# Taking the adding transfers out of the first MLP: every low half of its weights made by VectorE

## The chip, the core and the metric

One core of a Trainium2 chip runs the whole program. The metric is the device time of one execution, in microseconds (us), as the median over several executions. The engines are named as in the profile: PE (TensorE matmuls), PEld (TensorE weight loads), DVE (VectorE), ACT (ScalarE), POOL (GpSimd), SP (SyncE, which here only issues transfers).

## What is computed

The reference runs two two-layer transformer-like blocks one after the other on a sequence of 256 tokens of width 1024, all in float32. The part that matters here is the MLP of the first layer of the first block:

```python
h = rms_norm(x, norm_mlp[layer]) * (1.0 + scale2) + shift2
x = x + gate2 * (jnp.square(jax.nn.relu(h @ mlp_w1[layer])) @ mlp_w2[layer])
```

`mlp_w1` is 1024 x 4096 and `mlp_w2` is 4096 x 1024. The shifts, scales and gates of later layers come from `mod = c_act @ ada_w[layer] + ada_b[layer]`, whose dot products the kernel computes in between.

## The kernel before, in words

**Two halves of every number.** A matmul operand is held as a high half (float32 rounded to the type `fp32r`) and a low half (what the rounding lost). A product is the sum of three matmuls: high weight by high input, high weight by low input, low weight by high input. The low half of a weight is the loaded weight minus its high half.

**Weights.** They arrive in units of 128 x 2048 floats (1 MB), in one fixed order (`weight_plan`), through six buffers `raw0` to `raw5`. SP issues the loads in program order (`pump`, L369, L378), each into a buffer that was released (`release`, L392). `unit_ahead` (L397) splits a unit into a ring of three pairs of tiles: ACT writes the high half (`wh0` to `wh2`), DVE subtracts and writes the low half (`wl0` to `wl2`, L422, through the helper at L314), and then the raw buffer is released. So the ring lets a unit be split while PE still works on the two units ahead of it.

**Adding transfers.** For seven units of the first MLP (`DMALO`, L43: the units 0, 2, ... 12 of the second weight) the low half is made in another way (L407 to L413): ACT writes the high half, releases the raw buffer, writes minus the high half into the `wl` tile, and POOL issues a transfer that reads the weights from device memory a second time and adds them into that tile (L411).

**The first MLP** (`mlp`, L951, tag `m1`). `A(u)` multiplies the input by 256 columns of the first weight (48 matmuls) into PSUM. DVE then reduces two columns (`wb`, L334) and scales and shifts the result into `ht` (L327), ACT takes relu, square and the high half `hh`, DVE the low half `hl`. `B(u)` multiplies `hh` and `hl` by 256 rows of the second weight (48 matmuls, `rows_mm`, L506), summing over all u. PE's order is A0, A1, B0, A2, B1, A3, ..., A15, B13, and then B14 with B15 and the final evacuation. A unit that is split by an adding transfer is multiplied with `late=True`: all 32 matmuls with the high weights first, and then the 16 with the low weights.

**Side work.** While the MLP runs, DVE also computes 24 dot products of the modulation (`ada_next`, L687; two for each 1 MB unit, which are read from the same six raw buffers) and tables for a later state-space layer (`s5_tables`, `s5_turns`). They have a lower priority than the MLP's work. The order of the instructions on PE, DVE and ACT in this stage is set by a scheduler when the program is built; SP and POOL keep the program's order. Each engine runs its instructions in that order, and one that waits holds up all behind it.

Of the kernel before, what the change touches and what calls it, by code (L numbers as in the profile page):

```python
# [10 lines left out]
F32 = mybir.dt.float32  # L11
F32R = mybir.dt.float32r
U8 = mybir.dt.uint8
AF = mybir.ActivationFunctionType
# [6 lines left out]
ADD, SUB, MUL, MAX, MIN = ALU.add, ALU.subtract, ALU.mult, ALU.max, ALU.min  # L21

T = 256
D = 1024
NK = D // 128
# [13 lines left out]

DMALO = {("m1b", u) for u in range(0, 14, 2)}  # L43
S5SEQ = "g P0 P1 g T0 T1 TB0 M0 P2 P3 TB1 Q0 Q1 T2 T3 g Q2 Q3"


# [227 lines left out]
class Prog:  # L274
# [122 lines left out]
    def unit_ahead(self, ahead, between=None):  # L397

        last = min(self.used_n + ahead, len(self.wseq) - 1)
        while self.split_n <= last:  # L400
            j = self.wseq[self.split_n]
            if j not in self.slot:
                assert self.split_n > self.used_n, ("not loaded", self.plan[j][1])
                break
            b = self.split_n % len(self.hb)
            raw = self.raw_of(j)
            if self.plan[j][1] in DMALO:  # L407
                self.act(self.hb[b], raw, AF.Copy)
                self.release(j)
                self.act(self.lb[b], self.hb[b].bitcast(F32), AF.Copy, scale=-1.0)  # L410
                self.nc.gpsimd.dma_start(out=self.lb[b], in_=self.a["wst"][self.wpos[j]], accum_op=ADD)  # L411
                self.split_n += 1
                continue  # L413
            n = 1 + (self.plan[j][1][0] in HALVES)
            parts = [slice(i * 2048 // n, (i + 1) * 2048 // n) for i in range(n)]
            for c in parts:
                self.act(self.hb[b][:, c], raw[:, c], AF.Copy)
            if between is not None:
                between()
                between = None  # L420
            for c in parts:
                self.tt(self.lb[b][:, c], raw[:, c], self.hb[b][:, c].bitcast(F32), SUB)  # L422
            self.release(j)
            self.split_n += 1
        if between is not None:
            between()
# [76 lines left out]
                wh, wl = (t[:, k, m * 128:(m + 1) * 128] for t in (hv, lv))  # L503
                self.pair(outs[m], wh, wl, self.X2[S][:, k], k == 0, k == NK - 1)

    def rows_mm(self, units, xs, banks, start, stop, evac=None, late=False):  # L506

        kt = [(h, l, j) for h, l in units for j in range(2)]
        out = lambda m: self.pb[banks[m // 2]][:, (m % 2) * T:(m % 2 + 1) * T]
        if evac is not None:  # L510
            fin, a, b = evac
        if late:
            for q, m in [(q, m) for q in range(2) for m in range(NK)]:
                h, l, j = kt[q]
                w = h[:, j * D + m * 128:j * D + (m + 1) * 128]
                self.mm(out(m), w, xs[q][0], q == 0 and start and m % 2 == 0, False)
                self.mm(out(m), w, xs[q][1], False, False)
            for q, m in [(q, m) for q in range(2) for m in range(NK)]:
                h, l, j = kt[q]
                self.mm(out(m), l[:, j * D + m * 128:j * D + (m + 1) * 128], xs[q][0], False, q == 1 and stop and m % 2 == 1)  # L520
            return
        for m in range(NK):
            o = out(m)
            for q, (h, l, j) in enumerate(kt):
                c = j * D + m * 128
                xh, xl = xs[q]
                wh, wl = h[:, c:c + 128], l[:, c:c + 128]
                self.mm(o, wh, xh, q == 0 and start and m % 2 == 0, False)
                self.mm(o, wh, xl, False, False)
                self.mm(o, wl, xh, False, q == len(kt) - 1 and stop and m % 2 == 1)  # L530
            if evac is not None and m % 2 == 1:
                for i in (m - 1, m):
                    fin(i, out(i))
                    a(i)
                    if i:
                        b(i - 1)
        if evac is not None:
            b(NK - 1)
# [412 lines left out]
    def mlp(self, tag, S, finish, side=(), after=None, before=None):  # L951
        n = DFF // 256
        with self.tc.tile_pool(name="pm" + tag, bufs=1) as p:
            hh = [p.tile([128, 2, T], F32R, name=f"hh{i}") for i in range(3)]
            hl = [p.tile([128, 2, T], F32R, name=f"hl{i}") for i in range(3)]
            tt_ = [p.tile([128, 2, T], F32, name=f"ht{i}") for i in range(2)]
            wb = [p.tile([128, 2], F32, name=f"wb{i}") for i in range(2)]
            yb = (0, 1, 2, 3)

            def A(u):  # L960
                b = 4 + 2 * (u % 2)
                t = s = tt_[u % 2]
                ps = [self.pb[b], self.pb[b + 1]]
                self.proj_T((tag + "a", u), S, ps, n=258, parts=1 + (u == 0))
                if u == 0:
                    self.stats(6, std=True, r2=True)
                w = wb[u % 2]
                self.red(w, self.pball[:, b:b + 2, 256:258], ADD)
                for m in range(2):
                    self.stt(t[:, m, :], self.stdb, w[:, m:m + 1], ps[m][:, :T], MUL, ADD)  # L970
                self.act(t, t, AF.Relu)
                self.act(s, t, AF.Square)
                self.act(hh[u % 3], s, AF.Copy)
                self.tt(hl[u % 3], s, hh[u % 3].bitcast(F32), SUB)

            def B(us, fin=None):
                ws = [self.unit((tag + "b", u), ahead=2 - i) for i, u in enumerate(us)]
                xs = [(hh[u % 3][:, j, :], hl[u % 3][:, j, :]) for u in us for j in range(2)]
                self.rows_mm(ws, xs, yb, us[0] == 0, us[-1] == n - 1, fin, (tag + "b", us[0]) in DMALO)

            def sides(b):
                self.side_banks = (b, b + 1)
                for one in side:

                    while one:
                        g, budget = one[0]
                        start, said = self.vcost, "more"
                        while said == "more" and self.vcost - start <= budget:
                            said = next(g, "end")
                        if said != "end":  # L990
                            break
                        one.pop(0)

            A(0)
            for u in range(1, n - 1):
                A(u)
                sides(6 - 2 * (u % 2))
                if u == n - 2:
                    A(n - 1)
                B([u - 1])  # L1000
                sides(4 + 2 * (u % 2))
            for one in side:
                for g, _ in one:
                    for _ in g:
                        pass
            if after is not None:
                after()
            if before is not None:
                before()
            B([n - 2, n - 1], finish)  # L1010

    def mlp_finish(self, gate, nxt):
# [826 lines left out]
```

## Time and profile before

| | |
|---|---|
| median of 3 runs | 1299.5 us (1299.23 to 1301.8) |
| profiled execution, its own time | 1300.48 us |
| its span, first to last instruction | 1298.7 us |
| DVE, ACT busy over the span | 1006.0 us (77%), 693.4 us (53%) |
| first MLP, from PE's first matmul of its statistics to the first evacuation | 171.4 to 363.4 us |
| bytes of the adding transfers | 7.34 MB of 291.18 MB |

The profile is one execution on the chip. Its page gives the busy time of each engine and the costliest groups of instructions; the waits name who waited for whom; the timeline gives single instructions with the idle time before them; the windows give busy time and the granted TensorE clock (1.00 is 2.4 GHz, 0.50 is 1.2 GHz) in chosen stretches. Instructions overlap slightly at their ends, so what one takes from its engine is read from the start of one to the start of the next.

### The profile page before, as it was taken

How to read it: one execution, taken by the hardware profiler on the slowest of the kernel's cores; microseconds unless marked ns; L12 is line 12 of the kernel's file. 1: busy time of each engine (PE TensorE's matmuls, PEld its weight loads, DVE VectorE, ACT ScalarE, POOL GpSimd, SP SyncE). 2: the span in 40 equal slices, each digit the busy share in tenths (PEclk: the TensorE clock that was granted, in tenths of full speed). 3: DMA queues.
4: the chain of work that ended last, by engine and by line, in shares of the span. 5: the costliest groups of instructions: out<-in, count | busy, mean ns of one | idle time of the engine just before them, and what ended most of it. 6: DMA issues, size and time to landing. Idle time of an engine off the chain costs nothing.

```text
span 1298.7 us, 22539 instructions
## 1 busy us (share of the span) xinstructions
PE 1223.4 (94%) x9412; PEld 1136.2 (87%) x9412; DVE 1006.0 (77%) x1391; ACT 693.4 (53%) x891; POOL 91.5 (7%) x80
## 2 busy tenths in 40 slices
PE   2999989989998999999999799999999999999997
PEld 1999889989998889999999589887889999888886
DVE  7899989867799997899966756667656886877553
ACT  4545466655755885545554345455445554655442
POOL 0012120000020002000001204000000000100000
PEclk7999999999999999999999899999999999999999
DMA  9877579887875564888879795354545533455510
GB/s 383 330 269 282 212 260 310 269 291 248 278 277 227 200 248 170 314 280 284 257 268 223 150 378 186 138 185 163 212 179 211 193 114 131 161 181 183 219 68 33
DMA packets 64662, 291.18 MB, mean 224 GB/s; under 512 B 8112, under 2 KB 26032, under 8 KB 32048
## 3 DMA queue, kind: packets, MB, share of 16 engines
q1 hardware_dynamic: 63552, 282.40, 60.8%
q0 software_dynamic: 1008, 7.34, 2.8%
q8 instruction: 74, 1.21, 0.4%
q14 instruction: 28, 0.23, 0.1%
HBM read 275.04 MB, written 14.68 MB: 223 GB/s over the span
## 4 chain that ended last, share of the span: by engine, by line
PE 62%; DVE 18%; ACT 8%; DMA 7%; issue 4%; POOL 1%; DVEq 0%; ACTq 0%; POOLq 0%; SPq 0%
PE psall L337 61%; DMA wl<-in_wst_dram 7%; DVE wl L314 6%; ACT wh L294 4%; DVE raw L687 3%; PE psall L340 1%; DVE tmpn L327 1%; ACT wl L294 1%; DVE sqt L327 1%; DVE X L327 1%; DVE adaacc L314 1%; ACT X L294 1%; DVE td L314 1%; POOL sqat L565 1%; DVE tmpn L314 0%
## 5 line engine op out<-in xcount | busy, mean ns | idle before, releaser
L337 PE MATMUL psall<-X,wh 128*128 128x256 f32 (+2 forms) x3360 | 727.2, 308 | 28.7 <-ACT wh L294 21.4
L337 PEld LDWEIGHTS psall<-X,wh 128*128 128x128 f32 x3360 | 542.7, 191 | 68.0 <-ACT wh L294 21.8
L337 PE MATMUL psall<-X,wl 128*128 128x256 f32 (+1 forms) x1992 | 557.3, 283 | 5.6 <-DVE wl L314 5.6
L314 DVE TENSOR_TENSOR wl<-raw,wh 128x2048 fp32r<-128x2048 f32 (+1 forms) x225 | 410.4, 1841 | 104.7 <-ACT wh L294 99.6
L294 ACT ACTIVATE wh<-raw 128x2048 fp32r<-128x2048 f32 (+1 forms) x232 | 354.4, 1546 | 205.7 <-PE psall L337 183.4
L337 PEld LDWEIGHTS psall<-X,wl 128*128 128x128 f32 x1992 | 376.2, 190 | 12.0 <-DVE wl L314 11.2
L337 PE MATMUL psall<-hh,wl 128*128 128x256 f32 x512 | 130.9, 291 | 11.5 <-DMA wl<-in_wst_dram 11.5
L337 PE MATMUL psall<-hh,wh 128*128 128x256 f32 x512 | 140.5, 285 | 0.0
L337 PE MATMUL psall<-hl,wh 128*128 128x256 f32 x512 | 140.0, 283 | 0.4 <-DVE hl L314 0.4
L337 PE MATMUL psall<-hid,wh 128*128 128x512 f32 (+1 forms) x432 | 136.3, 372 | 0.0
L565 POOL TENSOR_TENSOR sqat<-sqat,sqt 128x256 f32<-128x256 f32 x52 | 56.5, 1087 | 886.3 <-ACT sqt L294 885.1
L337 PE MATMUL psall<-hid,wl 128*128 128x256 f32 x384 | 108.0, 281 | 0.3 <-DVE wl L314 0.3
L337 PEld LDWEIGHTS psall<-hh,wl 128*128 128x128 f32 x512 | 92.2, 196 | 14.1 <-DMA wl<-in_wst_dram 12.9
L337 PEld LDWEIGHTS psall<-hl,wh 128*128 128x128 f32 x512 | 97.9, 192 | 0.6 <-DVE hl L314 0.6
L337 PEld LDWEIGHTS psall<-hh,wh 128*128 128x128 f32 x512 | 97.6, 191 | 0.5 <-issue 0.4
L337 PEld LDWEIGHTS psall<-hid,wh 128*128 128x128 f32 x432 | 78.1, 189 | 15.4
L687 DVE CUSTOM_DVE_ANT_0 raw<-raw,adaacc,prmt 128x1024 f32<-128x1024 f32 x64 | 81.2, 1292 | 4.3 <-DMA raw<-in_wst_dram 4.3
L337 PEld LDWEIGHTS psall<-hid,wl 128*128 128x128 f32 x384 | 72.6, 189 | 0.6 <-DVE wl L314 0.6
L294 ACT ACTIVATE tmpn<-psall 128x256 f32<-128x256 f32 (+1 forms) x38 | 17.7, 465 | 62.1 <-PE psall L337 62.1
L314 DVE TENSOR_TENSOR tmpn<-tmpn,psall 128x256 f32<-128x256 f32 (+1 forms) x32 | 17.6, 552 | 38.0 <-ACT tmpn L294 38.0
L294 ACT ACTIVATE ht<-ht 128x512 f32<-128x512 f32 x64 | 39.9, 625 | 12.4 <-DVE ht L327 11.9
L687 DVE CUSTOM_DVE_ANT_0 raw<-raw,adaacc,adn 128x1024 f32<-128x1024 f32 x32 | 42.1, 1338 | 4.2 <-ACT td L294 4.2
(346 smaller groups left out, 1256.8 us busy)
## 6 DMA issues: line engine op xcount, KB each, us to landing
raw<-in_wst_dram SPq DMA_DIRECT2D x231, 1024.0 KB, 5.8
wl<-in_wst_dram POOLq DMA_DIRECT2D x7, 1024.0 KB, 12.6
dQ<-s5X SPq DMA_DIRECT2D x8, 512.0 KB, 4.8
dP<-s5X SPq DMA_DIRECT2D x16, 256.0 KB, 5.6
s5X<-in_wst_dram SPq DMA_DIRECT2D x4, 1024.0 KB, 14.3
raw<-dK SPq DMA_DIRECT2D x32, 128.0 KB, 9.5
s5X<-in_s5blk_dram SPq DMA_DIRECT2D x8, 256.0 KB, 3.8
s5X<-dP SPq DMA_DIRECT2D x2, 1024.0 KB, 8.0
```

What stands on the lines that cost most here:

```text
L294: i = self.nc.scalar.activation(out=out, in_=in_, func=func, **kw)
L314: return self.nc.vector.tensor_tensor(out=out, in0=a, in1=b, op=op)
L327: return self.nc.vector.scalar_tensor_tensor(out=out, in0=a, scalar=s, in1=b, op0=op0, op1=op1)
L337: return self.in_bank(out, self.nc.tensor.matmul(out, lhsT=l, rhs=r, start=start, stop=stop))
L340: return self.in_bank(out, self.nc.tensor.transpose(out, in_, self.ident))
L565: self.nc.gpsimd.tensor_tensor(out=self.sqa, in0=self.sqa, in1=s, op=ADD)
L687: self.nc.vector.tensor_tensor_reduce(out=w, in0=w, in1=self.crow, scale=1.0 if sc is None else sc, scalar=b, op0=MUL, op1=ADD, accum_out= ...
```

## The change

The set `DMALO` and the branch that serves it are removed, so the seven units take the ordinary way: ACT writes the high half, DVE subtracts, and the raw buffer is released after DVE's subtraction. With it go the argument `late` and its order of matmuls.

```diff
-DMALO = {("m1b", u) for u in range(0, 14, 2)}
...
-            if self.plan[j][1] in DMALO:
-                self.act(self.hb[b], raw, AF.Copy)
-                self.release(j)
-                self.act(self.lb[b], self.hb[b].bitcast(F32), AF.Copy, scale=-1.0)
-                self.nc.gpsimd.dma_start(out=self.lb[b], in_=self.a["wst"][self.wpos[j]], accum_op=ADD)
-                self.split_n += 1
-                continue
...
-    def rows_mm(self, units, xs, banks, start, stop, evac=None, late=False):
+    def rows_mm(self, units, xs, banks, start, stop, evac=None):
...
-        if late:
-            for q, m in [(q, m) for q in range(2) for m in range(NK)]:
-                h, l, j = kt[q]
-                w = h[:, j * D + m * 128:j * D + (m + 1) * 128]
-                self.mm(out(m), w, xs[q][0], q == 0 and start and m % 2 == 0, False)
-                self.mm(out(m), w, xs[q][1], False, False)
-            for q, m in [(q, m) for q in range(2) for m in range(NK)]:
-                h, l, j = kt[q]
-                self.mm(out(m), l[:, j * D + m * 128:j * D + (m + 1) * 128], xs[q][0], False, q == 1 and stop and m % 2 == 1)
-            return
...
-                self.rows_mm(ws, xs, yb, us[0] == 0, us[-1] == n - 1, fin, (tag + "b", us[0]) in DMALO)
+                self.rows_mm(ws, xs, yb, us[0] == 0, us[-1] == n - 1, fin)
```

The scheduler then orders this stage anew on PE, DVE and ACT; before and after the stage the orders are the same, and SP's is the same throughout. POOL loses its seven transfers in the stage. Line numbers in the changed kernel are smaller, by 2 (L312 for L314) up to 19.

PE at one of the seven units (B2, split into `wh0` and `wl0`; `hh2` and `hl2` are its inputs), before, at its end and the start of the next unit:

```order
L337 MATMUL psall_61<-hh2_1486,wh0_73 128x256
L337 MATMUL psall_61<-hl2_1489,wh0_73 128x256
L337 MATMUL psall_61<-hh2_1486,wl0_76 128x256 x16
L337 MATMUL psall_61<-X00_171,wh1_74 128x258
L337 MATMUL psall_61<-X00_171,wh1_74 128x256
L337 MATMUL psall_61<-X00_171,wl1_77 128x258
```

and now, at its start:

```order
L335 MATMUL psall_61<-X00_171,wl2_78 128x258
L335 MATMUL psall_61<-X00_171,wh2_75 128x258
L335 MATMUL psall_61<-X00_171,wh2_75 128x256
L335 MATMUL psall_61<-X00_171,wl2_78 128x258
L335 MATMUL psall_61<-hh2_1486,wh0_73 128x256
L335 MATMUL psall_61<-hl2_1489,wh0_73 128x256
L335 MATMUL psall_61<-hh2_1486,wl0_76 128x256
```

The low half was needed after 32 matmuls of its unit, and is now needed by the third.

ACT around the same kind of unit (B4, in `wh1`), before, with the relu and the square of the unit before it in `ht0`:

```order
L294 ACTIVATE wh1_74<-raw1_68 128x2048
L294 ACTIVATE ht0_1490<-ht0_1490 128x512
L294 ACTIVATE wl1_77<-wh1_74 128x2048
L294 ACTIVATE ht0_1490<-ht0_1490 128x512
L294 ACTIVATE hh1_1485<-ht0_1490 128x512
L294 ACTIVATE wh2_75<-raw0_67 128x2048
```

and now:

```order
L292 ACTIVATE wh1_74<-raw1_68 128x2048
L292 ACTIVATE ht0_1490<-ht0_1490 128x512 x2
L292 ACTIVATE hh1_1485<-ht0_1490 128x512
L292 ACTIVATE wh2_75<-raw0_67 128x2048
L292 ACTIVATE wh0_73<-raw4_71 128x2048
```

The copy with the sign changed is gone from between the two steps on `ht0`.

DVE from the reduction after A8 on (`wb0`), before; `ISA raw` is a dot product of the modulation, `ISA mod` its short second part, `wl1_77<-raw2_69` the low half for A10:

```order
L334 TENSOR_REDUCE wb0_1492<-psall_61 128x2
L687 ISA raw1_68,mod1_1_123<-raw1_68,adaacc1_136,adn1_1_130,prmt_88 128x1024
L687 ISA mod1_1_123 128x1
L327 SCALAR_TENSOR_TENSOR ht0_1490<-stdbt_106,wb0_1492,psall_61 128x256 x2
L687 ISA raw4_71,mod1_0_122<-raw4_71,adaacc1_136,prmt_88 128x1024
L687 ISA mod1_0_122 128x1
L687 ISA raw4_71,mod1_0_122<-raw4_71,adaacc1_136,prmt_88 128x1024
L687 ISA mod1_0_122 128x1
L314 TENSOR_TENSOR hl2_1489<-ht0_1490,hh2_1486 128x512
L314 TENSOR_TENSOR wl1_77<-raw2_69,wh1_74 128x2048
```

and now:

```order
L332 TENSOR_REDUCE wb0_1492<-psall_61 128x2
L325 SCALAR_TENSOR_TENSOR sqt_102<-adaacc0_135,sqt_102 128x512
L325 SCALAR_TENSOR_TENSOR ht0_1490<-stdbt_106,wb0_1492,psall_61 128x256 x2
L312 TENSOR_TENSOR wl0_76<-raw5_72,wh0_73 128x2048
L312 TENSOR_TENSOR hl2_1489<-ht0_1490,hh2_1486 128x512
L325 SCALAR_TENSOR_TENSOR tmpn_103<-adaacc0_135,tmpn_103 128x512
L668 ISA raw0_67,mod1_1_123<-raw0_67,adaacc1_136,adn1_1_130,prmt_88 128x1024
L668 ISA mod1_1_123 128x1
L312 TENSOR_TENSOR sqt_102<-sqt_102,tmpn_103 128x512
L668 ISA raw1_68,mod1_1_123<-raw1_68,adaacc1_136,adn1_1_130,prmt_88 128x1024
L668 ISA mod1_1_123 128x1
L312 TENSOR_TENSOR wl1_77<-raw2_69,wh1_74 128x2048
```

The added low half of B8 (`wl0_76<-raw5_72`) stands here, and side work that stood ahead of this reduction (the second dot product of `raw0`, the table steps on `sqt` and `tmpn`) now stands behind it.

## Rows read from the trace of the kernel before

**Rows 1.** The page, first part: busy us (share of the span) x instructions.

```profile
PE 1223.4 (94%) x9412; PEld 1136.2 (87%) x9412; DVE 1006.0 (77%) x1391; ACT 693.4 (53%) x891; POOL 91.5 (7%) x80
```

**Rows 2.** Windows: first MLP, its first part, then the second MLP (two stretches).

```profile
core 0: us, PE busy (x) PEld busy (x) DVE busy (x) ACT busy (x) POOL busy (x), PEclk, DMA share, GB/s
171.40:363.40 192.00, 179.87 (x1440) 177.99 (x1441) 151.92 (x276) 117.57 (x114) 6.33 (x8) 0.97 0.86 285
171.40:271.10 99.70, 92.79 (x733) 91.51 (x734) 85.12 (x179) 58.07 (x58) 3.76 (x5) 0.97 0.85 278
...
540.00:640.00 100.00, 100.00 (x879) 96.06 (x878) 97.84 (x95) 52.57 (x61) 0.00 (x0) 1.00 0.84 285
523.90:695.00 171.10, 171.10 (x1491) 165.32 (x1490) 146.64 (x148) 88.81 (x104) 0.00 (x0) 1.00 0.86 274
```

**Rows 3.** PE's waits, 165 to 372 us: us in total, times, longest.

```profile
PE psall L337 <- DMA wl<-in_wst_dram: 11.5, 7, 2.7
...
PE psall L337 <- DVE hl L314: 0.4, 1, 0.4
PE psall L337 <- DVE wl L314: 0.3, 1, 0.3
```

**Rows 4.** Chain of waits that ended last, 230 to 272 us: start, us, what.

```profile
222.25 12.86 DMA wl<-in_wst_dram
...
235.16 9.33 PE psall L337 x63
...
246.94 1.82 ACT wl L294
```

**Rows 5.** PE's timeline at two of the seven waits: start, us, group [idle before].

```profile
235.16 3.19 PE L337 MATMUL psall<-hh,wl 128*128 128x256 f32 x16 [2.01 <-DMA wl<-in_wst_dram]
...
339.82 2.17 PE L337 MATMUL psall<-hh,wl 128*128 128x256 f32 x16 [2.02 <-DMA wl<-in_wst_dram]
```

**Rows 6.** Windows at three stretches of low clock (columns as in rows 2).

```profile
235.96:239.36 3.40, 3.40 (x18) 3.40 (x17) 1.77 (x4) 3.32 (x4) 0.00 (x0) 0.50 0.87 349
263.60:266.70 3.10, 3.10 (x17) 3.10 (x17) 2.28 (x2) 0.00 (x0) 0.00 (x0) 0.51 0.44 172
290.20:293.90 3.70, 3.70 (x21) 3.70 (x21) 1.77 (x2) 1.92 (x3) 0.00 (x0) 0.54 1.01 423
```

**Rows 7.** DVE's timeline around A7's reduction: start, us, instruction.

```profile
255.03 1.34 DVE L687 CUSTOM_DVE_ANT_0 raw<-raw,adaacc,adn 128x1024 f32<-128x1024 f32 x1
256.30 0.08 DVE L687 DVE_READ_ACCUMULATOR2_ANT mod<- 128x1 f32 x1
...
256.71 0.86 DVE L327 SCALAR_TENSOR_TENSOR ht<-stdbt,wb,psall 128x256 f32<-128x256 f32 x2
257.49 0.42 DVE L322 TENSOR_SCALAR adaacc<-adaacc 128x512 f32<-128x512 f32 x1
257.98 2.29 DVE L314 TENSOR_TENSOR wl<-raw,wh 128x2048 fp32r<-128x2048 f32 x1
260.18 0.68 DVE L314 TENSOR_TENSOR hl<-ht,hh 128x512 fp32r<-128x512 f32 x1
```

**Rows 8.** ACT's timeline at one of the seven units.

```profile
246.33 0.62 ACT L294 ACTIVATE ht<-ht 128x512 f32<-128x512 f32 x1
246.85 1.91 ACT L294 ACTIVATE wl<-wh 128x2048 fp32r<-128x2048 f32 x1
248.65 0.62 ACT L294 ACTIVATE ht<-ht 128x512 f32<-128x512 f32 x1
```

**Rows 9.** DVE's timeline: two reductions in a row with no wait of PE between.

```profile
322.48 0.16 DVE L334 TENSOR_REDUCE wb<-psall 128x2 f32<-128x4 f32 x1 [2.99 <-PE psall L337]
...
334.00 0.16 DVE L334 TENSOR_REDUCE wb<-psall 128x2 f32<-128x4 f32 x1 [1.47 <-PE psall L337]
```

**Rows 10.** Transfers, 171.4 to 363.4 us: count, KB each, us to landing.

```profile
raw<-in_wst_dram SPq DMA_DIRECT2D x42, 1024.0 KB, 8.6
wl<-in_wst_dram POOLq DMA_DIRECT2D x7, 1024.0 KB, 12.6
```

## The prediction, made before the changed kernel was run

> **What bounds the kernel now.** The page first: PE is busy for 1223.4 of 1298.7 us [rows 1], so time can fall only where PE stands still or runs below full clock. The windows come next, over the stage that the change touches [rows 2]. From 171.4 to 363.4 us PE is busy for 179.87 of 192.00 us at a mean clock of 0.97, VectorE for 151.92 and ScalarE for 117.57, and the transfer engines for 0.86 of the time. Then PE's waits there [rows 3]: 11.5 us in seven waits for the adding transfers, the longest 2.7, and 0.7 us for VectorE. The chain of waits shows how one comes about [rows 4]: a transfer of 12.86 us, PE's matmuls, ScalarE's copy with the sign changed, and then the next transfer. A low half made in this way takes 1.9 us for the high half, 1.9 for the copy and 12.6 for the transfer [rows 8, 10], some 16.4 us. PE asks for it two units and 32 matmuls after it has freed the ring's tile: 11.5 + 3.8 = 15.4 us, with 11.52 us for two units [rows 9] and 0.12 for a matmul. So these units are late by construction. Last, the clock: after some of the waits PE runs at 1.2 GHz for 3.40, 3.10 and 3.70 us [rows 6].
>
> **The change, part by part.**
>
> *Waits removed.* The seven transfers go, and with them 11.5 us of PE's waits [rows 3]. PE's matmuls stay as many as they were, 48 for a unit in either order: nothing.
>
> *Clock.* The three slow stretches cost 3.40 x 0.50 + 3.10 x 0.49 + 3.70 x 0.46 = 4.9 us [rows 6]. Each follows one of the waits; yet of two equally long waits, 2.01 and 2.02 us, one is followed by such a stretch (16 matmuls take 3.19 us) and the other is not (2.17 us) [rows 5]. So the bounds of what comes back are 0 and 4.9. I take 4.9: the second MLP, where PE never stops for 171.10 us, runs at 1.00 throughout [rows 2].
>
> *VectorE gets seven subtractions.* One takes 2.20 us from the queue (257.98 to 260.18) [rows 7]: 7 x 2.20 = 15.4 us, so its work in the stage becomes 167.3 us, in some 175.6 us (192.0 - 16.4). That is tight, above all in the first part. Going down the new order with the durations of rows 7 and their like, I find 92.0 us of work between the reductions after A1 and A9, eight pairs of units, for which PE needs 8 x 11.52 = 92.2 us [rows 9]; in the old order it is 84.1. So there VectorE is full, and whatever it loses early it can't make up before the ninth pair, whose work is 8.5 us. What matters is whether PE notices. ScalarE may write a high half once PE has left the tile, two units ahead of the need: 11.5 - 1.9 - 2.2 = 7.4 us to spare for the low half. From the end of A(u) to B(u) there are also two units: 11.5 less reduction and `ht` (0.9), three steps of ScalarE (1.9), `hl` (0.7) and one low half in between (2.2) leaves 5.8 [rows 7, 8]. Walking down the queue I find VectorE 2 to 4 us behind PE through this stretch, which is inside both.
>
> *ScalarE loses seven copies*, 7 x 1.9 = 13.3 us [rows 8], each of which stood between relu and square: `hh` comes that much sooner there. It hides behind PE, so nothing by itself.
>
> *The loads.* A raw buffer of the seven is now released after VectorE's subtraction, not after ScalarE's first copy: 2.2 us later, plus VectorE's lag. Six buffers hold the loads that far ahead that 4 to 6 us mostly hide, and 7 of 49 transfers leave the queues [rows 10]. One place is thin. SP issues in order, and the load for B9 goes into `raw0`, whose second modulation product now stands behind a low half and `hl` of A8. By my walk it is issued about 14 us before B9 starts. If it lands within 6 us, ScalarE has the sines, B9's high half and `hh` of A9 done about 1 us ahead of PE; if it takes the 8.6 us of the median [rows 10], PE waits some 2 us.
>
> *New waits of PE.* The trace of before doesn't have this order, so I bound it: 0 as in the second MLP, whose units are all split in the ordinary way and where PE is busy for 171.10 of 171.10 us, with VectorE busy for 97.84 of 100.00 in the middle [rows 2]; 15.4 if all seven subtractions came onto the path. A gain below 0 is excluded but for the 0.7 us of rows 3. The second MLP is the nearest by far; for the thin place I take 2.0.
>
> The Trainium skill speaks against the change here: "Perfetto Trace Analysis", section "Identifying the Most-Contended Engine", holds that for VectorE the share of busy time is a fair measure of how near it is to its limit, and that the engine with the highest share is the one to relieve first. By that, loading VectorE further costs; the second MLP in this trace disagrees, and what the rule would make of the time is the first rival.
>
> *Sum.* The profiled execution took 1300.5 us (span 1298.7 and 1.8 around it), 1.0 more than the median. 1300.5 - 11.5 - 4.9 + 2.0 = 1286.1; against the median 1285.1. I say **1285**.
>
> **The rivals.**
>
> *A: VectorE sets the pace of the first part.* Up to 271.1 us it has 85.12 us of work [rows 2] and would get four subtractions: 93.9. PE is busy for 92.79 [rows 2], 3.2 of it owed to the first two slow stretches [rows 6], so it needs 89.6. If that work were not moved to later, 4.3 us would be lost, and with one slow stretch of 1.7 after such a wait the time is 1299.5 - 16.4 + 6.0 = 1289.1, up to 1292.5 with two more. For it: the full eight pairs. Against it: the new order has moved side work back, and the slack above. Chance 0.20. The rule of the Trainium skill's "Perfetto Trace Analysis" would make it this case.
>
> *B: the clock doesn't come back*, since the slow stretches have another cause or the new waits bring them on: 1299.5 - 11.5 + 2.0 = 1290.0. For it: the two equal waits of rows 5. Against it: full clock in the second MLP. Chance 0.08.
>
> *C: no change.* The weights' arrival sets the pace, at 0.86 of the transfer engines [rows 2], and what PE gains it waits for loads. Against it: no wait of PE ends with a load of `raw` [rows 3], and 7.34 MB less have to arrive. 1299.5. Chance 0.04.
>
> *D: slower.* VectorE works in order: a subtraction that waits for its high half, and so for PE, holds up `ht` and `hl` of the next unit behind it, and those hold up PE. If VectorE's idle time of 192.0 - 151.9 = 40.1 us [rows 2] came from that and stayed, the stage would last 151.9 + 15.4 + 40.1 = 207.4 us, so 1299.5 + 15.4 = 1314.9. It decides once VectorE's lag goes past 5.8 us. For it: the order was packed at building time by estimates. Against it: a lagging engine finds its inputs ready and stops idling, as in the second MLP with 2.16 us idle in 100 [rows 2]. Chance 0.06.
>
> **How the numbers follow.** My forecast has 0.62: from 1281.5 (no new waits, the 0.7 us gone too, rounded down) to 1288. The range 1281.5 to 1291.5 takes in A's centre and most of it, and B: about 0.85 by these cases, and I leave it there since the walk is by hand. A measurement of this kernel tells 0.2% (2.6 us) from no change; only C lies within, D is slower, everything else faster: 0.90, 0.04, 0.06.
>
> **What would show it.** In the profile of the changed kernel: no POOL transfers in the first MLP; PE's waits from 171 us to the first evacuation below 3 us, and those left on `hl`, `wl` or `wh`, around B9, if anywhere; clock 1.00 in the stage; the first evacuation at 346 to 350 us instead of 363.4; VectorE busy for about 167 us of some 177, near all of the time in its first half; later stages as before, only shifted. The forecast is wrong if PE waits for VectorE again and again (A: several waits of 1 to 3 us before 260 us; D: in every pair), if the clock is low without such waits (B), or if the evacuation is early but a later stage starts no sooner (C).

## The result, and the profile after

The changed kernel takes 1288.8 us (median of four runs, 1286.77 to 1291.04) beside 1300.65 us for the kernel before: ratio 0.9895, 95% interval 0.9877 to 0.9913. The medians differ by 11.8 us; the ratio by itself would make it 13.7 (11.3 to 16.0). Run again beside other kernels (run 11 below), it came to 1290.6 us and 0.9912 (0.9899 to 0.9925), where the medians differ by 11.9. So the gain is about 12 us, and 10 to 16 with both intervals. The forecast was 1285.

The profiled execution took 1287.9 us. First the page's first part, of the kernel after:

```profile
span 1286.1 us, 22524 instructions
PE 1220.1 (95%) x9412; PEld 1134.5 (88%) x9412; DVE 1019.5 (79%) x1398; ACT 681.1 (53%) x884; POOL 83.8 (7%) x73
```

Against [rows 1] VectorE has seven instructions and 13.5 us more, ScalarE seven and 12.3 us less, POOL 7.7 us less, and the span is 12.6 us shorter. The windows of the kernel after, for the first MLP, its first part, and the one stretch of low clock that is left (columns as in [rows 2]):

```profile
171.40:353.00 181.60, 178.64 (x1458) 178.02 (x1459) 167.17 (x286) 105.64 (x108) 0.45 (x2) 0.98 0.71 263
171.40:261.00 89.60, 89.19 (x741) 89.14 (x742) 88.95 (x177) 51.29 (x52) 0.45 (x2) 1.00 0.70 260
345.95:352.60 6.65, 6.16 (x28) 6.01 (x28) 2.56 (x5) 0.43 (x1) 0.00 (x0) 0.50 0.99 402
```

The second line is the one to look at: VectorE is busy for 88.95 of 89.60 us, and PE, beside it, for 89.19 at full clock; its missing 0.4 us lie before the stage's first matmul. An engine that works in order and is 99% busy holds nobody up there. PE's waits of the kernel after, 165 to 372 us (total, times, longest; the second opens the stage, the third lies behind it):

```profile
PE psall L335 <- ACT hh L292: 2.4, 1, 2.4
PE psall L335 <- POOL sqat L546: 1.8, 1, 1.8
PE psall L335 <- DVE sbg L320: 1.1, 1, 1.1
```

All seven waits of [rows 3] for adding transfers are gone; from the stage's start at 171.8 us to 344 us PE doesn't stop. One new wait stands in their place, for `hh`, at 346.44 in PE's timeline, and the low clock of the third window above begins in it:

```profile
346.44 1.22 PE L335 MATMUL psall<-hh,wh 128*128 128x256 f32 x4 [2.41 <-ACT hh L292]
```

What low clock costs is read from PE's timeline of the kernel after, at 1.2 GHz and then at full clock:

```profile
350.25 0.42 PE L335 MATMUL psall<-hl,wh 128*128 128x256 f32 x1
350.46 0.41 PE L335 MATMUL psall<-hh,wl 128*128 128x256 f32 x1
...
353.02 0.28 PE L335 MATMUL psall<-hl,wh 128*128 128x256 f32 x1
353.14 0.28 PE L335 MATMUL psall<-hh,wl 128*128 128x256 f32 x1
```

A matmul starts 0.21 us after the one before it instead of 0.12 (20 of them take 4.26 us from 348.12 on), so low clock takes 0.44 of PE's working time, not half. So the bill inside the stage is: 11.5 us of waits and 0.7 us of small ones removed [rows 3], 4.5 us of low clock removed (three stretches of some 3.4 us [rows 6], at 0.44), and 2.4 us of wait and 2.7 us of low clock new (the 6.16 us that PE works in the third window, at 0.44): 11.6 us gained. Measured between two points that both kernels share, the reductions on VectorE after A1 of the first MLP and after A15 of the second, in its timeline, before:

```profile
180.76 0.15 DVE L334 TENSOR_REDUCE wb<-psall 128x2 f32<-128x4 f32 x1
...
695.07 0.16 DVE L334 TENSOR_REDUCE wb<-psall 128x2 f32<-128x4 f32 x1 [0.99 <-PE psall L337]
```

and after:

```profile
179.51 0.16 DVE L332 TENSOR_REDUCE wb<-psall 128x2 f32<-128x4 f32 x1
...
682.28 0.16 DVE L332 TENSOR_REDUCE wb<-psall 128x2 f32<-128x4 f32 x1 [0.99 <-PE psall L335]
```

514.31 us have become 502.77: 11.5 us. The agreement is partly chance: these two points are VectorE's, and its new order brings A1's reduction 1.7 us nearer to the start of the stage. On PE, from the stage's first matmul to the start of its last (171.40 to 370.51 us before, 171.81 to 357.94 after), it is 13.0 us. Most of what the bill lacks is, by my estimate, a matter of counting: a matmul is recorded as 0.28 us long, but starts 0.12 after the one before it (lines above), so that idle time counted from its end leaves out 0.16 us at each wait, and nine waits have become one: 1.3 us. The stage begins 0.4 us later in the kernel after, and the whole span is 12.6 us shorter: nothing is won or lost behind the stage.

**What came out otherwise is the place of the new wait.** It is not B9, the thin place of the prediction, but the end: `hh` of A15. VectorE's timeline of the kernel after from 335 us:

```profile
335.45 2.29 DVE L312 TENSOR_TENSOR wl<-raw,wh 128x2048 fp32r<-128x2048 f32 x1
337.66 0.68 DVE L312 TENSOR_TENSOR sqt<-sqt,tmpn 128x512 f32<-128x512 f32 x1
338.26 0.69 DVE L312 TENSOR_TENSOR hl<-ht,hh 128x512 fp32r<-128x512 f32 x1
338.87 0.42 DVE L321 TENSOR_SCALAR sqt<-sqt 128x512 f32<-128x512 f32 x1
339.20 0.15 DVE L332 TENSOR_REDUCE wb<-psall 128x2 f32<-128x4 f32 x1
339.27 2.28 DVE L312 TENSOR_TENSOR wl<-raw,wh 128x2048 fp32r<-128x2048 f32 x1
341.47 0.86 DVE L325 SCALAR_TENSOR_TENSOR ht<-stdbt,wb,psall 128x256 f32<-128x256 f32 x2
```

and ScalarE's:

```profile
341.33 1.28 ACT L305 ACT_TABLE_LOAD   x1
342.63 1.91 ACT L292 ACTIVATE wh<-raw 128x2048 fp32r<-128x2048 f32 x1
344.45 1.27 ACT L292 ACTIVATE ht<-ht 128x512 f32<-128x512 f32 x2
345.75 0.63 ACT L292 ACTIVATE hh<-ht 128x512 fp32r<-128x512 f32 x1
```

PE is done with A15 at 335.3 us. Its reduction comes at 339.20, 3.9 us behind (A14's came 2.4 us behind, and those of A1 to A13 0.2 to 1.5), and `ht` waits for one more subtraction; then ScalarE has a table load and a split copy ahead of relu. `hh` is ready at 346.4, 11 us after the products. PE had work for 8.7 us (B13 and half of B14, up to 344.03) and stood for 2.4.

### The profile page after: what moved, and what is told of

Read it like the earlier page. It is cut to its first block, busy times and chain, and to the rows that moved or that the text cites. A ratio compares the mean times of both kernels' runs of the same rounds, so it can differ in the third digit from the quotient of the medians.

```text
span 1286.1 us, 22524 instructions
## 1 busy us (share of the span) xinstructions
PE 1220.1 (95%) x9412; PEld 1134.5 (88%) x9412; DVE 1019.5 (79%) x1398; ACT 681.1 (53%) x884; POOL 83.8 (7%) x73
## 4 chain that ended last, share of the span: by engine, by line
PE 66%; DVE 17%; ACT 8%; DMA 4%; issue 3%; POOL 1%; SPq 0%; DVEq 0%; ACTq 0%; POOLq 0%
PE psall L335 65%; DVE wl L312 6%; ACT wh L292 5%; DVE raw L668 3%; DMA raw<-in_wst_dram 2%; DMA raw<-dK 2%; PE psall L338 1%; DVE tmpn L325 1%; DVE X L325 1%; DVE sqt L325 1%; DVE td L312 1%; DVE sqt L312 1%; DVE xTt L312 1%; DVE tmpn L312 0%; ACT tmpn L292 0%
## 5 line engine op out<-in xcount | busy, mean ns | idle before, releaser
L312 DVE TENSOR_TENSOR wl<-raw,wh 128x2048 fp32r<-128x2048 f32 (+1 forms) x232 | 426.9, 1857 | 100.8 <-ACT wh L292 100.1
L335 PEld LDWEIGHTS psall<-X,wl 128*128 128x128 f32 x1992 | 375.2, 189 | 11.3 <-DVE wl L312 10.6
L335 PE MATMUL psall<-hh,wh 128*128 128x256 f32 x512 | 145.8, 288 | 2.4 <-ACT hh L292 2.4
L335 PE MATMUL psall<-hh,wl 128*128 128x256 f32 x512 | 146.1, 286 | 0.0
L335 PE MATMUL psall<-hl,wh 128*128 128x256 f32 x512 | 145.9, 286 | 0.0
L335 PEld LDWEIGHTS psall<-hh,wl 128*128 128x128 f32 x512 | 99.3, 194 | 1.2 <-issue 1.2
L335 PEld LDWEIGHTS psall<-hid,wh 128*128 128x128 f32 x432 | 78.1, 189 | 15.4
L312 DVE TENSOR_TENSOR tmpn<-tmpn,psall 128x256 f32<-128x256 f32 (+1 forms) x32 | 17.6, 552 | 38.0 <-ACT tmpn L292 38.0
```

The costliest lines, as they stand in the source:

```text
L312: return self.nc.vector.tensor_tensor(out=out, in0=a, in1=b, op=op)
L335: return self.in_bank(out, self.nc.tensor.matmul(out, lhsT=l, rhs=r, start=start, stop=stop))
```

## The experiments

Three theories went into the runs. **Theory 1**: the adding transfers were late by construction; without them PE's waits and the low clock behind them go, and VectorE takes the subtractions because it runs behind PE by less than the slack. **Theory 2**: VectorE is, or nearly is, what sets the pace, and what was not won is its lag. **Theory 3**: the gain is a by-product, of the other order of the products (3a), of ScalarE's freed time (3b) or of the saved traffic (3c). The kernel before was measured beside them: 1302.5 us for runs 1 to 4, 1302.8 for 5 to 8, 1302.4 for 9 to 11.

**Run 1: the old order of the products.** The branch for the adding transfers is taken out of `unit_ahead`, all else stays as before:

```
-            if self.plan[j][1] in DMALO:
-                ...
-                continue
```

> The seven low halves come from VectorE as in the changed kernel, but the products of these units keep the order of the kernel before (all products with the high half first, the low half's last). Theory 1 (the adding transfers arrived too late and PE stood waiting for them; the order was only there to soften that): 1288.8 us within 1.5, no waits for the low halves, clock 1.00 up to A15. Theory 3a (part of the gain comes from the new order of the products): 3 us or more above the changed kernel.

Measured: 1289.9 us, ratio 0.9903 (0.9881 to 0.9925); no wait for a low half, one of 3.7 us for `hh` of A15. The order of the products is worth nothing that can be measured here: 3a falls. Run 1 is also the changed kernel's stand-in for runs 2 to 4 on the same chip.

**Run 2: ScalarE's copies put back.**

```
+SEV = {("m1b", u) for u in range(2, 16, 2)}
...
+            if self.plan[j][1] in SEV:
+                self.act(self.dump, self.hb[b].bitcast(F32), AF.Copy, scale=-1.0)
```

> The changed kernel with ScalarE's seven negated copies put back (seven 128 x 2048 copies, each 1.9 us, 13.3 us in all, into a tile that nobody reads). Theory 1: ScalarE was about 60% busy in the stage, so within 2 us of 1288.8; if anything the wait for hh of A15 (2.4 us in the changed kernel) grows. Theory 3b (the gain is ScalarE's freed time): back by most of the gain, 1297 or more.

Measured: 1293.7 us, 0.993 (0.9907 to 0.9953), 3.8 us above run 1: more than theory 1 allowed, far from 3b. PE's waits of run 2, 172 to 366 us:

```profile
PE psall L336 <- DVE hl L313: 3.3, 2, 1.7
PE psall L336 <- POOL sqat L549: 1.8, 1, 1.8
PE psall L336 <- ACT hh L293: 0.9, 1, 0.9
PE psall L336 <- DVE wl L313: 0.4, 1, 0.4
```

All but the second, which opens the stage in every run, lie behind 326 us. My "hides behind PE, so nothing by itself" holds for the stage's body only: at A14 and A15 ScalarE is in the chain. But the price is not clean. The edit puts the copies at the units 2, 4, ... 14, while the kernel before had them at 0, 2, ... 12; the copy for unit 14 ran at 339.66 us, between relu and square of A14, where there had been none. The intervals of runs 1 and 2 overlap, too.

**Run 3: the traffic put back, its result unused.**

```
+SEV = {("m1b", u) for u in range(2, 16, 2)}
...
+            if self.plan[j][1] in SEV:
+                self.nc.gpsimd.dma_start(out=self.dump, in_=self.a["wst"][self.wpos[j]])
             self.release(j)
```

> The changed kernel with seven plain 1 MB transfers from POOL's queue, one per even unit, into a tile that nobody reads: the traffic of the adding transfers without their result. Theory 1: 1288.8 us within 2 (the loads of raw may land some 2 to 4 us later, which only the wait for hh of A15 could feel). Theory 3c (the gain is the 7.3 MB less of traffic): 1296 or more.

Measured: 1296.2 us, 0.9945 (0.9925 to 0.9966), 6.3 us above run 1: a miss for theory 1, and 3c's number (1296 or more). From A1 to the second MLP's A15 the profiled executions differ by less, 507.4 us against 504.9 in run 1.

The edit doesn't bring back the old traffic, though. Nothing holds a transfer back but the one before it, and POOL issued all seven early (durations in ns, first and last start in us):

```profile
L416 POOL DMA_DIRECT2D dump<-in_wst_dram x7: 530/530/722, 173.8 to 223.1; - x7
```

In the kernel before the adding transfers were issued from 174.7 to 327.3 us. So the run prices 7 MB packed into some 50 us, in the part of the stage where VectorE is full. In VectorE's timeline of run 3 a modulation product now waits for its load (no such wait in the kernel after):

```profile
201.06 1.28 DVE L671 CUSTOM_DVE_ANT_0 raw<-raw,adaacc,prmt 128x1024 f32<-128x1024 f32 x1 [2.72 <-DMA raw<-in_wst_dram]
```

What that means for an engine without reserve is in the first 94 us of the stage, first in run 3, then in the kernel after, then before:

```profile
173.86:267.86 94.00, 94.00 (x781) 93.95 (x782) 89.57 (x180) 52.01 (x52) 3.97 (x8) 1.00 0.85 326
```
```profile
171.81:265.81 94.00, 94.00 (x781) 93.95 (x782) 93.31 (x183) 54.16 (x56) 0.04 (x1) 1.00 0.67 248
```
```profile
171.40:265.40 94.00, 87.09 (x690) 85.81 (x691) 80.33 (x173) 56.69 (x55) 3.76 (x5) 0.97 0.88 291
```

In run 3 VectorE does 3.7 us less in the same time, at transfer engines busy for 0.85 instead of 0.67. Its reductions stay 3 to 4 us later than in the kernel after to the end of the stage, and PE meets that in waits of 1.6 us for `wl` at 328.76 and 3.2 us for `hh` at 352.13. Before, VectorE had 13.7 us to spare in this stretch, and PE waited for nothing of the kind. What the removed traffic, at its own times, would have cost the changed kernel no run shows. Against 3c as the whole cause stand the seven waits of [rows 3], which were for the result of these transfers, and run 7.

**Run 4: each new subtraction twice.**

```
+SEV = {("m1b", u) for u in range(0, 14, 2)}
...
+            if self.plan[j][1] in SEV:
+                self.tt(self.lb[b], raw, self.hb[b].bitcast(F32), SUB)
             self.release(j)
```

> The changed kernel with each of the seven new subtractions done twice (15.4 us more on VectorE, same result). Theory 1 (VectorE is nearly full, but runs behind PE by less than the slack, which takes up part of it): VectorE has 88.95 us of work in the first 89.6 us; four of the seven lie there and add 8.8 us, of which some 3 us of slack are left, so PE waits about 6 us and catches up no more than that, plus up to 4 us of slow clock behind waits: 1292 to 1299. Theory 2 (VectorE sets the pace of the stage already): the whole 15.4 us and the clock, 1304 or more. If VectorE had room to spare: 1289.

Measured: 1303.2 us, 1.0 (0.9988 to 1.0012), 13.3 us above run 1: between theory 1's upper end and theory 2. PE's waits of run 4 (172 to 372 us), then its windows:

```profile
PE psall L336 <- ACT wh L293: 5.3, 2, 4.9
PE psall L336 <- ACT hh L293: 3.7, 2, 3.6
PE psall L336 <- DVE wl L313: 2.7, 3, 1.6
```
```profile
172.57:266.57 94.00, 93.79 (x775) 93.33 (x776) 93.30 (x167) 54.66 (x55) 0.04 (x1) 1.00 0.67 248
266.57:336.57 70.00, 62.08 (x491) 60.97 (x489) 66.73 (x100) 33.74 (x34) 0.00 (x0) 0.95 0.64 237
```

For 94 us PE still runs through, with four more subtractions on VectorE. That isn't slack being used up: VectorE does 167 instructions there instead of 183, since the new order has put side work back, and up to A10 its reductions come at most 1.4 us behind PE's products. Then PE stands for 11.7 us. The longest wait, 4.9 us for `wh` at 289.56, comes by way of a load that SP could issue only when a modulation product gave back its buffer, at 281.0 us; it landed at 287.5. Of SP's waits in run 4, 240 to 300 us:

```profile
SPq L377 <- DVE mod L671: 24.7, 1, 24.7
```

In the kernel after the longest such wait is 12.7 us. Of 15.4 us put on VectorE 13.3 came out at the end. VectorE has next to no room left in the changed kernel, less than I expected (some 3 us of slack and half of the cost absorbed); how large its reserve is the run doesn't tell, since late hand-overs, late loads and some 5 us of low clock are mixed in the 13.3.

**Run 5: the write-outs off SP's queue.** In the kernel after ScalarE waits for loads of `raw` (18.6 us, seven times, against 3.3, twice, before), because SP issues them behind the side work's write-outs. Was that why `hh` of A15 came late?

```
-            L.do(nc.sync.dma_start, out=tb[:, o:o + 512], in_=flat(C))
+            L.do(nc.gpsimd.dma_start, out=tb[:, o:o + 512], in_=flat(C))
```

(and so for the other three `dma_start` lines of `s5_tables` and `s5_turns`)

> The changed kernel with the side work's write-outs (dW, dM, dTB) issued from POOL's queue instead of SP's. Theory 1 (what was not won is one wait of 2.4 us for hh of A15 and 3.4 us of slow clock behind it; hh is late because ScalarE waits for raw, and raw is late because SP issues its loads behind the write-outs that wait for the side work): ScalarE's waits for raw fall from 18.6 us to under 9, the wait and the slow stretch go, 5.8 us below the changed kernel, ratio to the kernel before about 0.985. Theory 2 (hh of A15 is late because VectorE is too full to serve it): no change, ratio 0.9895 within 0.002.

Measured: 1292.9 us, 0.9921 (0.9893 to 0.995). ScalarE's waits for `raw` in run 5 (172 to 352 us) are:

```profile
ACT wh L292 <- DMA raw<-in_wst_dram: 0.4, 1, 0.4
```

The loads come in time, and PE still waits 3.5 us for `hh` of A15, with low clock behind it. So late loads were real and were not why `hh` came late: that part of theory 1 falls. (The scheduler also laid out VectorE's side work anew, with a wait of 1.2 us for `hl` at 308.7, so the run is no clean price of the queue.)

**Run 6: no side work between A14 and A15.**

```
-                sides(6 - 2 * (u % 2))
-                if u == n - 2:
+                if u < n - 2:
+                    sides(6 - 2 * (u % 2))
+                else:
                     A(n - 1)
```

> The changed kernel with the slice of side work between A14 and A15 left to the slice behind B13. Theory 2 (side work on VectorE and ScalarE just ahead of A15 holds up hh of A15): the wait of 2.4 us and its slow clock go, ratio 0.985. Theory 1 (the weights are late on SP's queue, which stays): the wait stays or shrinks by less than 1 us, ratio 0.9895 within 0.002.

Measured: 1291.4 us, 0.9909 (0.9884 to 0.9934), a wait of 2.5 us for `hh`. The scheduler laid out the same queues all the same: on VectorE around A15's reduction a subtraction before it and one behind, on ScalarE the sines, the table load and the copy ahead of relu. The edit moved nothing there, so the run says nothing about theory 2.

**Runs 7 and 8: adding transfers for some units only.**

```
-DMALO = {("m1b", u) for u in range(0, 14, 2)}
+DMALO = {("m1b", u) for u in range(0, 6, 2)}
```

(run 7; `range(6, 14, 2)` in run 8)

> The kernel before with the adding transfers kept for units 0, 2 and 4 alone. Theory 1 (each unit costs its own wait of the trace of before and the slow clock behind it): about 4.5 us of waits (0.96 and 2.01 for units 0 and 4, some 1.5 for unit 2) and one slow stretch of 1.7 us over the changed kernel: 6 us of the 11.8 us come back, ratio 0.994. Theory 3 (traffic or an engine's sum of work decides): three sevenths, ratio 0.994 too; so this run tells them apart only with the next.

> The kernel before with the adding transfers kept for units 6, 8, 10 and 12 alone. Theory 1: waits of 1.78, 2.68, 0.52 and 2.02 us and two slow stretches of 1.6 us, 10.2 us over the changed kernel, less the 5.8 us of the wait at A15 that the kernel before did not have: between 4 and 10 us over the changed kernel, ratio 0.993 to 0.997, and no wait of PE up to unit 6 at clock 1.00. Theory 3: four sevenths of the 11.8 us, 6.7 us, ratio 0.9947. The trace decides: theory 1 wants the waits for wl at these four units, each within 1 us of the kernel before's.

Measured: run 7 1291.9 us, 0.9922 (0.9897 to 0.9948), as fast as runs 5 and 6, measured beside it; run 8 1303.0 us, 1.0002 (0.9986 to 1.0019), as slow as the kernel before. Run 7's interval still holds the forecast of 0.994, run 8's doesn't hold its 0.993 to 0.997. By the trace the price by unit fails in both. In run 7 (PE's waits, 172 to 372 us) the three transfers cost less than before:

```profile
PE psall L337 <- DMA wl<-in_wst_dram: 2.6, 3, 1.3
PE psall L337 <- DVE hl L314: 1.9, 2, 1.5
PE psall L337 <- ACT hh L294: 1.1, 1, 1.1
```

No stretch of low clock follows any of them, at unit 4 neither (1.12 us of wait, against 2.01 in [rows 5]), nor the shorter wait at A15: the 2.7 us of low clock that the changed kernel has, and run 7 hasn't, make up for most of its 3.4 us more of waits in the stage. In run 8 PE waits for two of the four transfers (2.1 us at unit 6, 3.9 at unit 10), for those of units 8 and 12 not at all, and anew elsewhere: 2.0 for `hl`, 1.6 for `wh`, 2.5 for `wl`, 1.6 for `hh`. Behind the wait for `wh`, at 336.6 us, stands SP's queue, in the timeline of run 8:

```profile
316.50 0.33 SPq L1356 DMA_DIRECT2D dTB<-tmpn  x1
323.09 0.33 SPq L1356 DMA_DIRECT2D dTB<-sqt  x1
323.51 0.38 SPq L1356 DMA_DIRECT2D dM<-adaacc  x1
323.94 2.96 SPq L378 DMA_DIRECT2D raw<-in_wst_dram  x3
```

Two write-outs whose sines come late stand ahead of three loads for 7 us, and ScalarE then waits for one of these:

```profile
334.67 1.91 ACT L294 ACTIVATE wh<-raw 128x2048 fp32r<-128x2048 f32 x1 [9.78 <-DMA raw<-in_wst_dram]
```

So here the queue seems to cost, which it did not at A15 of the changed kernel (run 5); no run tested it by itself. Theory 3's sevenths fail as well: neither the count of transfers nor their traffic orders runs 7 and 8. That it is what else stands in the queues at that time fits the trace, and isn't tested.

**Run 9: A15's evacuation first.** The one that asks theory 2 about the wait that is left:

```
+OFF = 60
...
+                with (self.tc.high_priority(offset=OFF) if tag == "m1" and u == n - 1 else nullcontext()):
+                    self.red(w, self.pball[:, b:b + 2, 256:258], ADD)
...
+                    self.act(hh[u % 3], s, AF.Copy)
```

> The changed kernel with the first evacuation of A15 (reduction, ht, relu, square, hh) given priority over the subtractions for units 14 and 15 on VectorE and over a split copy and the sines on ScalarE; everything else in its old order. After run 5 theory 1's weights are ruled out (ScalarE waited 0.4 us for raw there and PE still 3.5 us for hh). Theory 2' (VectorE runs some 4 us behind PE at A15: A15's products end at 335.3, its reduction comes at 339.2 and its ht at 341.5 behind a subtraction, and ScalarE then has a copy ahead of it): hh of A15 is done by about 341, the wait of 2.4 us and the slow stretch go, 3 to 6 us below the changed kernel in the same call. Rival: the subtraction for unit 14, now behind, is late in its place: a wait for wl of 1 to 3 us, no gain.

Measured: 1287.6 us (1285.49 to 1293.16), 0.9895 (0.9876 to 0.9913), beside 1290.6 for the changed kernel (run 11): 3 us less at the median, with intervals that overlap. The cause of the wait is shown by the trace. VectorE's timeline of run 9:

```profile
334.24 0.16 DVE L334 TENSOR_REDUCE wb<-psall 128x2 f32<-128x4 f32 x1 [0.25 <-PE psall L337]
...
335.64 0.47 DVE L327 SCALAR_TENSOR_TENSOR ht<-stdbt,wb,psall 128x256 f32<-128x256 f32 x1
```

and PE's, in the same run:

```profile
341.89 0.51 PE L337 MATMUL psall<-hh,wh 128*128 128x256 f32 x2 [0.83 <-ACT hh L294]
...
358.38 0.38 PE L337 MATMUL psall<-X,wh 128*128 128x256 f32 x1 [0.88 <-DVE sbg L322]
361.71 1.21 PE L337 MATMUL psall<-sqat,onesd 128*128 128x256 f32 x2 [1.74 <-POOL sqat L548]
```

The reduction and `ht` no longer stand behind two subtractions, and relu not behind the table load and the copy; `hh` is ready 7.8 us behind A15's products instead of 11.2. The wait is 0.8 instead of 2.4 us, although PE's own order asks for `hh` sooner here (7.0 us behind the products instead of 8.7), and the clock stays full: from the stage's first matmul to the first evacuation it is 176.9 us (171.03 to 347.92) instead of 179.8 in the kernel after (171.81 to 351.56). But PE then comes early to the border of the next stage, waits there for the norm's squares from POOL, and the low clock comes there instead, for some 6.8 us of this window (its mean is 0.56):

```profile
361.10:368.80 7.70, 7.09 (x32) 6.91 (x33) 5.42 (x8) 3.30 (x6) 0.55 (x1) 0.56 0.80 279
```

In the profiled execution all of it was given back (A1 to the second MLP's A15: 178.72 to 683.48, 504.8 us, against 502.8 in the kernel after and 504.5 in run 11). Run 9 is the fastest of the study, but whether it beats the changed kernel is not settled.

**Run 10: run 9 with the traffic of run 3.**

> The kernel of run 9 with the seven plain 1 MB transfers of run 3. If the traffic in run 3 cost through hh of A15 alone (its waits for hh were 3.5 us against 2.4): within 1.5 us of run 9. If the traffic has a price of its own (loads of raw that land later and hold up ScalarE and VectorE elsewhere): 3 to 5 us above run 9.

Measured: 1294.2 us, 0.9945 (0.9928 to 0.9961), 6.6 us above run 9 (5.0 us from A1 to the second MLP's A15, in the profiled executions). So the traffic, packed into the first 55 us of the stage as in run 3, has a price of its own: the same product on VectorE waits 3.04 us for its load at 198.60, and PE waits for `hh` at 284.1 (1.16 us) and for `wl` at 327.6 (1.64).

**Run 11: the changed kernel again.**

> The changed kernel itself, beside the two others on the same chip, so that they can be compared with it: ratio to the kernel before 0.9895 within 0.002, one wait of some 2.4 us for hh of A15 and a slow stretch of 6 to 7 us behind it.

Measured: 1290.6 us, 0.9912 (0.9899 to 0.9925), with 3.4 us of wait for `hh` and low clock from 347.8 to 354.6 us. The ratio is within the bound given; the wait was 1 us longer than in the first profile.

## Why the prediction was right, and where it was not

*Waits removed, 11.5 us.* Right: none is left.

*Clock, 4.9 us.* Right for the three stretches, which went with their waits. Mis-sized a little: I took half of their time, and the rows give 0.44, so 4.5 us. It was a fair call between bounds of 0 and 4.9; what I didn't carry on is that a new wait can bring its own. The 2.0 us that I took for new waits had no clock behind them; the one that came took 2.7. Rival B had said it ("the new waits bring them on", 1290.0, chance 0.08), and came true in part: 1288.8 lies nearer to its figure than to 1285, and 0.8 above the 1288 at which my own case ended. The range holds it because it was drawn to take in A and B.

*VectorE.* 167.3 us of work were forecast, 167.17 found [rows 7 give the 2.20 for each]; it is full up to A9, and no wait of PE comes from it there: as the trace shows. That it would be 2 to 4 us behind PE through this stretch is not: its reductions come 0.2 to 1.5 us behind the products up to A13 (A7's, the latest of them up to A9, starts at 249.93 us, and its products end at 248.42), and only at A14 and A15 2.4 and 3.9. Rival A is refuted: it wanted waits of PE before 260 us, and PE stood nowhere before 344. That the measured 1288.8 falls on its 1289.1 is a coincidence; the time alone could not have told A, B and my own case apart. The rule named from the Trainium skill's "Perfetto Trace Analysis", section "Identifying the Most-Contended Engine", isn't refuted with it: the section judges TensorE not by its busy matmuls but by its arithmetic rate and the busy share of its weight loads. In this stretch these loads are busy for 89.14 us and VectorE for 88.95 (second window above), so that the rule finds the two level.

*New waits, 2.0 us "around B9".* The size was near (2.4) by luck; the place was wrong, and the clock behind it missing. The step that failed is the sentence "From the end of A(u) to B(u) there are also two units". It holds while units alternate; but the last two B follow B13 at once, so A15 has one unit and the half of B14, 8.7 us in place of 11.5. With VectorE 3.9 us behind, a subtraction of 2.3 us ahead of `ht`, and ScalarE's table load and copy ahead of relu, that is 2.4 us too few. Run 9 puts A15's evacuation ahead of these, and the wait shrinks to 0.8; how much of that is VectorE's order and how much ScalarE's it doesn't tell. At B9 itself nothing was late.

*ScalarE's copies: "nothing by itself".* For the gain, yes: run 2 stayed 9 us below the kernel before. Whether copies at the old places would have cost the changed kernel anything stays open (3.8 us with one of them at A14).

*Loads.* SP's order behind the side work did delay them, as feared, later than at B9 (waits of ScalarE of up to 5.7 us), and PE didn't notice (run 5). I left the 7.34 MB out of the sum but for an argument against rival C. Seven further transfers cost the changed kernel some 6 us by the medians when they come early and close together (runs 3 and 10; 2.5 and 5.0 in the profiled executions). So the change probably works in part because it frees the transfer engines for the loads that VectorE now can't wait for; that is argued, not shown.

*The sum.* The forecast's 11.5 + 4.9 - 2.0 = 14.4 us stand against 12.5 between the two profiled executions. The terms: 2.7 us of low clock behind the new wait, 0.4 for the old low clock, 0.4 for the longer wait, and a stage that began 0.4 us later, less 0.7 for the small waits and 1.3 for what the count of idle time leaves out. (The range's lower end, 1281.5, is 0.9 below what its own terms give: 1285.1 - 2.0 - 0.7 = 1282.4.)

*The signs.* No POOL transfers, waits of PE below 3 us, VectorE's 167 us and the later stages came out as said. The clock was 0.98 in the stage and not 1.00, the wait that was left was for `hh`, which I hadn't listed, and the first evacuation came at 351.56 us, behind the 346 to 350.

Left open: what the removed traffic at its own times would cost the changed kernel; and why the stages up to 171 us differ by up to 3 us between runs whose code is the same there.

## What to carry to other kernels

When work moves from a late transfer to a full engine, count the slack of each hand-over by itself, the last ones of the loop first, where the order changes and nothing follows that could hide a lag. An engine at 99% in order is no bound while its lag is below the slack, but it has lost its reserve: here 15.4 us more on it cost 13.3 (run 4), by way of late loads too, since the work that was put back held their buffers. Price a removed wait with the low clock behind it, and a new one too. And when a run puts something back to price it, read from its trace whether it came back at the same place and time.

## What the runs showed of the hardware

The length of a wait does not tell whether the clock drops after it. In the kernel before, two waits of 2.0 us differed in that [rows 5]. After, 2.41 us came with 6.65 us at 1.2 GHz, about twice as long as a stretch of [rows 6] (3.1 to 3.7 us); in run 7 waits of 1.12 and 1.08 us were followed by none, and in run 8 one of 2.08 us by none; in run 9 a wait of 0.83 us by none, and 0.88 and 1.74 us, 3.3 us apart, by 6.8 us. At 1.2 GHz a 128x256 matmul started every 0.21 us, at full clock every 0.12. A drop thus cost about 1.5 us in the kernel before, and 2.7 us in the kernel after, there more than the 2.4 us of the wait.
